# A recorder that orders a hybrid attention and DeltaNet step by a model of the engines: TensorE charged with other times

## The chip, the cores and the metric

One core of one Trainium2 chip. The metric is the device time of one execution in microseconds (us), the median of three runs. Engines: PE is TensorE, PEld its weight loads, DVE VectorE, ACT ScalarE, POOL GpSimd, SP the queue that issues DMAs.

## The reference

Two layers of a diffusion backbone over 128 context tokens and 1024 latent tokens (together 1152), D_MODEL 1024. The core of a layer:

```python
h = rms_norm(x, p['norm_g']) * (1.0 + scale) + shift
cq, ckv, kpe, gate_a, b_in, c_in, x_in, gate_b, q_in, k_in, v_in, z, a_f, a_b, b_f, b_b, merge_g = split_columns(h @ p['w_in'])
o_a = mla_attention(q_nope, q_rope, k_nope, k_rope, v) * jax.nn.silu(gate_a)
o_b = conv_branch(b_in, c_in, x_in, gate_b, p['conv_b_w'])
o_c = gdn_branch(q_in, k_in, v_in, z, a_f, a_b, b_f, b_b, h0, p)
m = s_a * (o_a @ p['w_pa']) + s_b * (o_b @ p['w_pb']) + s_c * (o_c @ p['w_pc'])
x = x + res_gate * (m @ p['w_o'])
```

`gdn_branch` is a gated delta rule in chunks of 64 tokens, eight heads, forward and backward. Its scan is a chain in which each step needs the state of the step before:

```python
def step(state, xs):
    u_i, w_i, qd_i, kd_i, at_i, gl_i = xs
    v_new = u_i - jnp.einsum('bhck,bhkv->bhcv', w_i, state)
    o_i = jnp.einsum('bhck,bhkv->bhcv', qd_i, state) + jnp.einsum('bhij,bhjv->bhiv', at_i, v_new)
    state = state * jnp.exp(gl_i)[..., None, None] + jnp.einsum('bhck,bhcv->bhkv', kd_i, v_new)
    return state, o_i
```

## The kernel before

Every value is float32; large products are split into two parts of a shorter format and made of three products (`mm3s`). A layer has three parts: the *front* (input projection, convolutions, delta rule, then the projections of the attention's queries, keys and values), the *attention* (order written out by hand, with four projection tiles as fill), and the *mix* (gates, branch projections, output projection, and the start of the next layer).

In start, front and mix the order on the engines is not written out. Each job is a stream, a generator that yields one instruction at a time (`s_ip`, `s_ga`, `s_gc`, ...). A recorder, `Flow`, holds for each engine the time at which its model thinks the engine free (`free`), and for each buffer when it was last read or written (`log`). In `run` it takes, over and over, the stream whose next instruction can start first (`max(free, ready)`, with 0.02 us per rank on top); among instructions of the same engine one of a lower rank number goes first if its wait is short. `put` then books the instruction's time and issues it. The program that comes out is fixed: each engine works through its list in order, and waits where an operand is late. The model is used while the program is built alone.

The streams that matter here:

- `ip` (rank 9, the last): the input projection, 42 tiles of 128 columns (38 in the front, the last four in attention) by three token blocks of 384, 24 whole products (128x128 by 384 columns) each. A tile is named by its place: `ip0_18_2` is layer 0, tile 18, block 2. It is what PE does when nothing else is ready. `s_w` loads and splits its weights, `s_ev` takes its results out.
- `gc` (rank 3): the chain of the scan. Jobs 0 to 3 are pairs of heads of the latent tokens with 16 steps each, job 4 the context with 2 steps. A step is four products of 64x64 by 64 columns `p1` (a state `SH` into `p1`), three DVE operations into `scr`, four `pv`, one DVE operation, four `pk`, and two DVE operations into the next `SH`. On the chip each of these products shows as two MATMUL records (x8 for four products), and the profile writes `p1` as `p`.
- `ga`, `gb`, `gz` (ranks 7, 6, 4): what a job needs ahead of its chain: decay masks (`gm`, `sg`), Gram matrices (`G`), a triangular solve of 31 steps on DVE and POOL (`tmp`, `X`), and its last part on PE (`pw`). `gd` (rank 4): the outputs (`oi`, `oa`, `ot`).
- `lb`, `ln`, `w2`: after the chains, in the tail of the front: norms (`rs_kv`, `rs_cq`) and projections `ukp`, `uvp`, `uqp`, with what is left of `ip`.

Before, PE's time of an instruction was `op.c` of `cost` alone: columns / 2400 us for a whole product of 256 columns and more, 64/1200 or 64/600 us for a 64x64 one:

```python
            if ins[0].ap[0][1] <= 64:
                t = ins[0].ap[-1][1] / (1200.0 if out.offset // out.ap[0][0] else 600.0)
            return t
```

Of the kernel before, what the change touches and what calls it, by code (L numbers as in the profile page):

```python
# [39 lines left out]


class Op:
    __slots__ = ("e", "f", "r", "w", "c", "m")


class Wait:
# [9 lines left out]
def _span(ap):  # L56
    dims = ap.ap
    if ap.space == DRAM:
        lo, p0, p1 = ap.offset, 0, 1
        rest = dims  # L60
    else:
        ps, pn = dims[0]
        p0, lo = ap.offset // ps, ap.offset % ps
        p1 = p0 + pn
        rest = dims[1:]
    hi = lo + 1
    for s, n in rest:
        if s > 0:
            hi += s * (n - 1)
        else:  # L70
            lo += s * (n - 1)
    return p0, p1, lo, hi


def _free(ap):
    n = 1
    for _, k in ap.ap[1:]:
        n *= k
    return n


class Eng:
# [7 lines left out]
    def __getattr__(self, m):  # L90
        real = getattr(self.real, m)

        def call(*a, **kw):
            if not self.k.rec:
                return real(*a, **kw)  # L95
            op = Op()
            op.e = self.e
            op.f = lambda: real(*a, **kw)  # L98
            aps = [x for x in a if hasattr(x, "tensor")]
            out = kw.get("out")  # L100
            outs = [out] if out is not None else [aps.pop(0)]
            if kw.get("accum_out") is not None:
                outs.append(kw["accum_out"])
            ins = aps + [v for n, v in kw.items() if n not in ("out", "accum_out") and hasattr(v, "tensor")]
            if m == "matmul" and not kw.get("start", True):
                ins.append(outs[0])
            op.w = [(self.k.key(x), _span(x)) for x in outs]
            op.r = [(self.k.key(x), _span(x)) for x in ins]
            op.c = self.cost(m, outs[0], ins, kw)
            op.m = ins[0].ap[-1][1] / 1200.0 if self.e == "PE" else 0.0  # L110
            return op

        return call

    def cost(self, m, out, ins, kw):
        n = max([_free(out)] + [_free(x) for x in ins if x.space != DRAM]) if self.e != "PE" else _free(out)
        if self.e == "PE":
            if m == "transpose":
                return n * 2 / 2400.0
            r = ins[1].dtype == F32R  # L120
            t = n * ((1 if n >= 256 else 4) if r else 4) / 2400.0
# [3 lines that stand above are left out]
        if self.e == "DVE":  # L125
            return (0.131 if m == "scalar_tensor_tensor" else 0.065) + n / (160.0 if m == "reciprocal" else 960.0)
        if self.e == "ACT":
            return (0.307 if ins and ins[0].space != PSUM and n > 256 else 0.13) + n / 1600.0
        if self.e == "POOL":
            if kw.get("op") == ALU.pow:  # L130
                return 0.15 + n * 0.175
            return (0.15 if m != "tensor_tensor" else 0.1) + n / (1200.0 if m != "tensor_tensor" else 475.0)
        run = 1 << 30
        for x in [out] + ins:
            c = 1
            for st, k in reversed(x.ap[0 if x.space == DRAM else 1:]):
                if st != c:
                    break
                c *= k
            run = min(run, c)  # L140
        return out.nbytes() / 360e3 * (2 if run < 128 else 1)


class Flow:
# [8 lines left out]
    def __init__(self, k):  # L153
# [3 lines left out]
        self.ev = set()  # L157
        self.pace = {}

    def ready(self, op):  # L160
        t = 0.0
        for lst, wr in ((op.r, False), (op.w, True)):
            for key, (p0, p1, lo, hi) in lst:
                ps = key[0] == "P"
                for q0, q1, l2, h2, end, eng, w in self.log.get(key, ()):
                    if eng != op.e and ps:

                        hit = (q0 // 32 < -(-p1 // 32) and p0 // 32 < -(-q1 // 32) and l2 // 512 <= (hi - 1) // 512
                               and lo // 512 <= (h2 - 1) // 512)
                    else:  # L170
                        hit = (w or wr) and q0 < p1 and p0 < q1 and l2 < hi and lo < h2
                    if hit:
                        end += self.LAG[eng, op.e]
                        if end > t:
                            t = end
        return t

    def note(self, op, end):
        for lst, w in ((op.r, False), (op.w, True)):
            for key, sp in lst:  # L180
# [5 lines left out]
                if len(recs) > 96:  # L186
                    recs.sort(key=lambda x: x[4])
                    del recs[:32]

    def put(self, op, s):  # L190
        f = self.free
        if op.e == "SP":
            f["SP"] = s + 0.06
            hw = max(s, f.get("HW", 0.0))
            f["HW"] = hw + 0.45
            d = max(hw + 1.1, f.get("DMA", 0.0))
            f["DMA"] = d + op.c
            self.note(op, d + op.c)
        else:
            if op.e == "PE":  # L200
                s = max(s, f.get("PEW", 0.0) + op.m)
                f["PEW"] = s
            f[op.e] = s + op.c
            self.note(op, s + op.c)
        op.f()

    def step(self, st):
# [22 lines left out]
    def run(self, streams, until=None, evs=()):  # L230

        for n, s in streams.items():
            if "head" not in s:
                s.update(head=None, end=False, wait=None)
        names = sorted(streams, key=lambda n: streams[n]["rank"])
        while True:
            moved = True
            while moved:
                k0 = len(self.ev)
                for n in names:  # L240
                    self.step(streams[n])
                moved = len(self.ev) != k0
            if all(streams[n]["end"] for n in (names if until is None else until)) and all(e in self.ev for e in evs):
                return
            cand = []
            for n in names:
                op = streams[n]["head"]
                if op is not None:
                    cand.append((max(self.free.get(op.e, 0.0), self.ready(op)), streams[n]["rank"], n, op))
            if not cand:  # L250
                raise RuntimeError("streams wait for each other: %s" % {n: streams[n]["wait"] for n in names})
            best = min(cand, key=lambda x: (x[0] + 0.02 * x[1], x[1]))
            for x in cand:
                if x[3].e == best[3].e and x[1] < best[1]:
                    wait = x[0] - best[0]
                    if wait <= 0 or wait < self.WIN and wait < self.PREF * (best[3].c - wait):
                        best = x
                        break
            streams[best[2]]["head"] = None
            self.put(best[3], best[0])  # L260
# [9 lines left out]
class Kern:  # L270
# [618 lines left out]
    def conv_put(self, c, put):  # L889
        RA, RB = self.cbuf["RA"], self.cbuf["RB"]  # L890
        if c == 0:
            yield put(RA[:, 1:129], 0, 128)
            yield put(RA[:, 131:387], 128, 384)
        elif c == 1:
            yield put(RA[:, 387:580], 0, 193)
            yield put(RB[:, 0:193], 191, 384)
        else:
            yield put(RB[:, 193:577], 0, 384)
# [1652 lines left out]
```

## Time and profile before

| | |
|---|---|
| median of 3 runs | 3540.32 us (3534.69 to 3552.49) |
| the profiled execution's own time | 3544.98 us |
| its span, first to last instruction | 3543.2 us |
| instructions | 65525 |
| PE busy | 3375.9 us, 95% |
| mean granted TensorE clock | 0.97 |

The span is cut by what PE does: start to 112 us, front of layer 0 to 957 us, attention and mix to 1850 us, front of layer 1 to 2692 us, then attention and mix again. The granted clock is a share of full speed, 1.0 (2.4 GHz) or 0.5 (1.2 GHz) at any time.

### The profile page before, as it was taken

The numbers are of one execution on the slowest core, as the hardware profiler recorded it, in microseconds if no ns is written. First come the engines' busy times: TensorE is split into PE (matmuls) and PEld (weight loads), VectorE is DVE, ScalarE is ACT, GpSimd is POOL, SyncE is SP. The second block draws the span as 40 slices with busy tenths as digits, with TensorE's granted clock in tenths as the row PEclk, the third lists the DMA queues.
The fourth block names the chain that finished last, engine by engine and source line by source line (L and its number), as shares of the span: only waits on it lengthen the run. The fifth ranks groups of instructions, "written<-read, shape, count | busy, mean of one in ns | idle before, by whom it ended". The sixth has DMA issues, their size and how long they took to land. (4 is left out here: it accounts for less than half of the span.)

```text
span 3543.2 us, 65525 instructions
## 1 busy us (share of the span) xinstructions
PE 3375.9 (95%) x24654; PEld 2903.7 (82%) x24654; DVE 2310.6 (65%) x5052; ACT 1187.1 (34%) x2551; POOL 1538.9 (43%) x1550
## 2 busy tenths in 40 slices
PE   7999999999899999999999999999998999999998
PEld 4988777778765699999999877777788658999998
DVE  4467776774566488856664777786455665833755
ACT  4432222223334333332444232122242443333233
POOL 3156546533157544424212645654322774444231
PEclk9999899999999999999999989999999999999999
DMA  5333213213733235466333223122256322434842
GB/s 190 98 100 77 55 54 83 59 57 122 230 83 79 51 110 162 145 203 195 123 103 107 74 75 83 47 57 73 71 187 188 73 64 70 135 100 129 256 143 87
DMA packets 381339, 389.64 MB, mean 110 GB/s; under 512 B 162016, under 2 KB 310176, under 8 KB 380640
## 3 DMA queue, kind: packets, MB, share of 16 engines
q1 hardware_dynamic: 381024, 385.46, 36.5%
q8 instruction: 195, 3.19, 0.4%
q14 instruction: 120, 0.98, 0.1%
HBM read 264.54 MB, written 120.72 MB: 109 GB/s over the span
## 5 line engine op out<-in xcount | busy, mean ns | idle before, releaser
L98 PE MATMUL ip<-h,wh_wi 128*128 128x384 f32 x5328 | 1170.5, 358 | 3.6 <-DVE gb L98 1.1
L98 PEld LDWEIGHTS ip<-h,wh_wi 128*128 128x128 f32 x5328 | 932.8, 194 | 60.1 <-issue 16.4
L95 POOL TENSOR_TENSOR acc<-acc,P 128x512 f32<-128x512 f32 x224 | 289.1, 1291 | 126.1 <-ACT P L95 110.1
L98 POOL TENSOR_TENSOR tmp<-M,X 128x2 f32<-128x2 f32 (+30 forms) x310 | 218.6, 705 | 283.4 <-DVE X L98 263.1
L95 DVE TENSOR_REDUCE mx<-s 128x1 f32<-128x384 f32 (+1 forms) x400 | 209.2, 544 | 163.9 <-PE s L95 154.5
L95 ACT ACTIVATE P<-st 128x512 f32<-128x512 f32 x292 | 173.5, 598 | 264.9 <-PE st L95 229.3
L95 PE MATMUL st<-q,K 97*128 97x512 f32 (+1 forms) x912 | 257.2, 393 | 0.0
L98 POOL TENSOR_TENSOR sl<-ss,sl 128x512 fp32r<-128x512 f32 x100 | 144.3, 1444 | 245.7 <-ACT sl L98 227.6
L98 POOL TENSOR_TENSOR wh_wi<-wri,wh_wi 128x512 fp32r<-128x512 f32 x112 | 151.9, 1366 | 155.4 <-ACT wh_wi L98 151.6
L98 PE MATMUL pp<-ob,wp 128*128 128x384 f32 x1152 | 204.1, 336 | 2.2 <-DVE ob L98 1.8
L98 DVE TENSOR_REDUCE X<-tmp 128x1 f32<-128x2 f32 (+30 forms) x620 | 184.6, 319 | 31.4 <-POOL tmp L98 23.6
L98 PEld LDWEIGHTS pp<-ob,wp 128*128 128x128 f32 x1152 | 199.1, 188 | 6.6 <-POOL ob L98 3.7
L98 PE MATMUL wop<-h,wh_wo 128*128 128x384 f32 x1152 | 202.9, 335 | 0.0
L98 PE MATMUL sg<-h,sl 128*128 128x288 f32 x1440 | 201.1, 296 | 0.1
L98 PEld LDWEIGHTS wop<-h,wh_wo 128*128 128x128 f32 x1152 | 199.7, 188 | 1.1
L98 PEld LDWEIGHTS sg<-h,sl 128*128 128x128 f32 x1440 | 194.4, 188 | 0.3 <-POOL sl L98 0.3
L98 POOL TENSOR_TENSOR mU<-mU,mt 128x384 f32<-128x384 f32 x96 | 112.6, 1173 | 182.0 <-DVE mt L98 182.0
L98 ACT ACTIVATE VT<-pv,sst 128x64 f32<-128x64 f32 x256 | 66.7, 311 | 365.4 <-DVE scr L98 349.1
L95 PEld LDWEIGHTS st<-q,K 97*128 97x128 f32 x912 | 164.0, 190 | 28.3 <-issue 11.5
L98 POOL TENSOR_TENSOR gm<-g,cst 128x256 fp32r<-128x256 f32 x144 | 107.1, 754 | 162.0 <-PE sg L98 126.3
L98 DVE TENSOR_TENSOR tmp<-M,X 128x2 f32<-128x2 f32 (+30 forms) x310 | 162.5, 524 | 18.3 <-POOL M L98 12.5
L98 DVE SCALAR_TENSOR_TENSOR ada<-wada,cs,ada 128x256 f32<-128x256 f32 x224 | 148.9, 703 | 23.2 <-DMA wada<-in_w_ada 20.7
(339 smaller groups left out, 6327.4 us busy)
## 6 DMA issues: line engine op xcount, KB each, us to landing
wri<-in_w_in SPq DMA_DIRECT2D x160, 256.0 KB, 3.4
mt<-mD SPq DMA_DIRECT2D x144, 192.0 KB, 2.9
wada<-in_w_ada SPq DMA_DIRECT2D x128, 128.0 KB, 2.3
wrp<-in_w_p SPq DMA_DIRECT2D x48, 256.0 KB, 3.6
mD<-C SPq DMA_DIRECT2D x80, 144.0 KB, 1.9
mD<-cu SPq DMA_DIRECT2D x80, 144.0 KB, 1.8
ss<-in_w_in SPq DMA_DIRECT2D x40, 256.0 KB, 4.0
ws<-in_w_in SPq DMA_DIRECT2D x40, 256.0 KB, 4.3
```

The source lines that it names most:

```text
L95: return real(*a, **kw)
L98: op.f = lambda: real(*a, **kw)
```

## The change

`Flow` no longer books `op.c` for a product, but what the new `product` says: columns / 2400 + 0.013 us from 256 columns up (at least `op.c` where that is over 0.15), 0.03, 0.08 or 0.112 us for smaller ones; 0.1 us more where a product with fewer than 128 rows or columns of weights follows one with 128, or the other way round; and twice as much where the model's interval before held less than a share `SLOW` of full work. `low`, a rule of choice, is added but is off with `LOW = 0.0`. Nothing is computed otherwise than before, and no instruction is added or removed.

```diff
@@ -40,7 +40,7 @@
 
 
 class Op:
-    __slots__ = ("e", "f", "r", "w", "c", "m")
+    __slots__ = ("e", "f", "r", "w", "c", "m", "u")
 
 
 class Wait:
@@ -108,6 +108,9 @@
             op.r = [(self.k.key(x), _span(x)) for x in ins]
             op.c = self.cost(m, outs[0], ins, kw)
             op.m = ins[0].ap[-1][1] / 1200.0 if self.e == "PE" else 0.0
+            if self.e == "PE":
+
+                op.u = (ins[0].ap[0][1], ins[0].ap[-1][1], _free(outs[0]))
             return op
 
         return call
@@ -157,6 +160,8 @@
         self.ev = set()
         self.pace = {}
 
+        self.win, self.part, self.last = {}, False, None
+
     def ready(self, op):
         t = 0.0
         for lst, wr in ((op.r, False), (op.w, True)):
@@ -186,6 +191,42 @@
                 if len(recs) > 96:
                     recs.sort(key=lambda x: x[4])
                     del recs[:32]
+
+    GRID = 3.41
+    SLOW = 0.35
+    LOW = 0.0
+    SWITCH = 0.1
+    NEAR = 0.1
+
+    @staticmethod
+    def load(op):
+
+        k, m, n = op.u
+        part = k < 128 or m < 128
+        return k * m / 16384.0 * n / 2400.0, n / 2400.0 + 0.013 if n >= 256 else 0.03 if n <= 32 else 0.08 if part else 0.112, part
+
+    def low(self, op, s):
+
+        u, t, part = self.load(op)
+        if t > 0.15 or op.w[0][0] == self.last:
+            return False
+        return u + sum(x for e, x in self.recent if e > s + t - self.GRID) < self.LOW * self.GRID
+
+    recent = ()
+
+    def product(self, op, s):
+
+        u, t, part = self.load(op)
+        t = max(t, op.c) if t > 0.15 else t
+        if part != self.part:
+            t += self.SWITCH
+        self.part, self.last = part, op.w[0][0]
+        w = int(s / self.GRID)
+        if w > 1 and self.win.get(w - 1, 0.0) < self.SLOW * self.GRID:
+            t *= 2
+        self.win[w] = self.win.get(w, 0.0) + u
+        self.recent = [x for x in self.recent if x[0] > s - self.GRID] + [(s + t, u)]
+        return s + t
 
     def put(self, op, s):
         f = self.free
@@ -200,8 +241,11 @@
             if op.e == "PE":
                 s = max(s, f.get("PEW", 0.0) + op.m)
                 f["PEW"] = s
-            f[op.e] = s + op.c
-            self.note(op, s + op.c)
+                f["PE"] = self.product(op, s)
+                self.note(op, f["PE"])
+            else:
+                f[op.e] = s + op.c
+                self.note(op, s + op.c)
         op.f()
 
     def step(self, st):
@@ -254,6 +298,12 @@
                 if x[3].e == best[3].e and x[1] < best[1]:
                     wait = x[0] - best[0]
                     if wait <= 0 or wait < self.WIN and wait < self.PREF * (best[3].c - wait):
+                        best = x
+                        break
+            if self.LOW and best[3].e == "PE" and self.low(best[3], best[0]):
+
+                for x in cand:
+                    if x[3].e == "PE" and x[0] <= best[0] + self.NEAR and self.load(x[3])[1] > 0.15:
                         best = x
                         break
             streams[best[2]]["head"] = None
```

What that does to the order is seen in three places. First PE in layer 0, job 2, the step 5 of its chain up to step 6 (`p_2_5` is `p1` of job 2, step 5; `ip_27_0` is tile 27, block 0; `sg_4_1` belongs to job 4; the numbers at the end count buffers). Before:

```order
L98 MATMUL p_2_5_6396<-SH_2_1_6076,kTb_2_5437 64x64
L98 MATMUL ip_27_0_6352<-h,wh_wi_27_6017 128x384 x7
L98 MATMUL pv_2_5_6395<-scr_2_6072,ZT_0_968 64x64
L98 MATMUL sg_4_1_6321<-gm_4_1_10_6377,mr 128x256
L98 MATMUL pv_2_5_6395<-scr_2_6072,ZT_1_969 64x64
...
L98 MATMUL ip_27_0_6352<-h,wh_wi_27_6017 128x384 x4
L98 MATMUL pk_2_5_6435<-scr_2_6072,kt_2_5442 64x64 x4
L98 MATMUL sg_4_1_6321<-gm_4_1_11_6421,mr 128x256
L98 MATMUL ip_27_0_6352<-h,wh_wi_27_6017 128x384 x2
L98 MATMUL ip_27_1_6451<-h,wh_wi_27_6017 128x384
L98 MATMUL p_2_6_6447<-SH_2_0_6075,kTb_2_5437 64x64
```

The same place now:

```order
L98 MATMUL p_2_5_5288<-SH_2_1_5112,kTb_2_4829 64x64
L98 MATMUL ip_18_2_4989<-h,wh_wi_18_3156 128x384 x2
L98 MATMUL pv_2_5_5287<-scr_2_5108,ZT_0_968 64x64
L98 MATMUL pv_2_5_5287<-scr_2_5108,ZT_1_969 64x64
...
L98 MATMUL ip_18_2_4989<-h,wh_wi_18_3156 128x384
L98 MATMUL ip_19_0_5303<-h,wh_wi_19_4403 128x384 x2
L98 MATMUL pk_2_5_5319<-scr_2_5108,kt_2_4835 64x64 x4
L98 MATMUL ip_19_0_5303<-h,wh_wi_19_4403 128x384
L98 MATMUL p_2_6_5328<-SH_2_0_5111,kTb_2_4829 64x64
```

The fourteen `ip` products and two `sg` of the step have become six `ip`, and the `ip` tile at this place is number 18 and 19 instead of 27: the chain stands earlier against the projection.

Second DVE in the same step (`scr` and `SH` are the chain's, `tmp` and `X` the triangular solve of job 3, `YA` and `YB` the convolutions). Before:

```order
L98 TENSOR_TENSOR scr_2_6072<-p_2_5_6396,sst_2_5532 128x128
L98 TENSOR_REDUCE X_3_5802<-tmp_3_5803 128x10
L98 TENSOR_TENSOR scr_2_6072<-scr_2_6072,vT_2_5438 64x128 x2
L98 TENSOR_TENSOR tmp_3_5803<-M_3_5801,X_3_5802 128x210
...
L98 TENSOR_TENSOR scr_2_6072<-pv_2_5_6395,sst_2_5532 128x128
...
L98 TENSOR_TENSOR tmp_3_5803<-M_3_5801,X_3_5802 128x242
L98 SCALAR_TENSOR_TENSOR SH_2_0_6075<-SH_2_0_6075,egl_1096,pk_2_5_6435 128x64
L98 SCALAR_TENSOR_TENSOR SH_2_1_6076<-SH_2_1_6076,egl_1096,pk_2_5_6435 128x64
```

Now:

```order
L98 TENSOR_TENSOR scr_2_5108<-p_2_5_5288,sst_2_4896 128x128
L98 TENSOR_TENSOR scr_2_5108<-scr_2_5108,vT_2_4830 64x128 x2
L98 TENSOR_TENSOR scr_2_5108<-pv_2_5_5287,sst_2_4896 128x128
L98 SCALAR_TENSOR_TENSOR SH_2_0_5111<-SH_2_0_5111,egl_1092,pk_2_5_5319 128x64
L98 SCALAR_TENSOR_TENSOR SH_2_1_5112<-SH_2_1_5112,egl_1092,pk_2_5_5319 128x64
L98 SCALAR_TENSOR_TENSOR YA_962<-RA_960,sm_122,YA_962 128x578 x2
```

Job 3's solve has left job 2's chain; in the chains of jobs 0 and 1 the next job's solve still stands.

Third PE in the tail of layer 0's front, at the first `uqp`. Before, no `ip` was left there:

```order
L98 MATMUL uqp_6_0_9730<-qn_0_8989,w_6_9611 128x384 x9
L98 MATMUL uqp_6_1_9744<-qn_1_8990,w_6_9611 128x384 x9
L98 MATMUL uqp_6_2_9762<-qn_2_8991,w_6_9611 128x384 x9
L98 MATMUL uqp_7_0_9781<-qn_0_8989,w_7_9717 128x384 x9
L98 MATMUL uqp_7_1_9795<-qn_1_8990,w_7_9717 128x384 x9
```

Now:

```order
L98 MATMUL uqp_6_0_9630<-qn_0_8658,w_6_9436 128x384 x9
L98 MATMUL ip_37_0_9615<-h,wh_wi_37_9385 128x384 x8
L98 MATMUL uqp_6_1_9662<-qn_1_8659,w_6_9436 128x384 x9
L98 MATMUL ip_37_0_9615<-h,wh_wi_37_9385 128x384 x13
L98 MATMUL ip_37_1_9688<-h,wh_wi_37_9385 128x384 x10
L98 MATMUL uqp_6_2_9706<-qn_2_8660,w_6_9436 128x384 x9
```

When the delta rule's last output stands on PE, 2305 of layer 0's 2736 `ip` products have been issued where it was 2560; in layer 1 it is 2414 where it was 2775.

## Rows read from the trace of the kernel before

**Rows 1.** The page's first part: busy us, share of the span, instructions.
```profile
PE 3375.9 (95%) x24654; PEld 2903.7 (82%) x24654; DVE 2310.6 (65%) x5052; ACT 1187.1 (34%) x2551; POOL 1538.9 (43%) x1550
```
**Rows 2.** Windows: PE, PEld, DVE, ACT, POOL busy us, clock, DMA share, GB/s.
```profile
112.00:957.00 845.00, 798.50 (x7186) 668.47 (x7185) 564.32 (x1504) 251.79 (x632) 378.14 (x455) 0.95 0.31 90
```
**Rows 3.** Windows over the eight chains, columns as above.
```profile
335.90:433.40 97.50, 93.19 (x755) 69.94 (x755) 71.53 (x169) 26.65 (x71) 50.16 (x53) 0.79 0.12 31
...
711.30:784.40 73.10, 69.24 (x695) 51.03 (x696) 53.82 (x177) 14.43 (x47) 25.56 (x34) 1.00 0.17 51
...
2318.10:2396.20 78.10, 73.56 (x746) 55.37 (x746) 68.11 (x208) 16.75 (x53) 44.45 (x57) 1.00 0.08 24
...
sum 659.70, PE 626.59 PEld 469.69 DVE 519.07 ACT 148.84 POOL 321.85; mean PE 78.32 PEld 58.71 DVE 64.88 ACT 18.60 POOL 40.23
```
**Rows 4.** The same windows, `ip` alone: PE, PEld, DVE, ACT; counts add up to 1487.
```profile
335.90:433.40 97.50, 56.75 (x187) 37.08 (x186) 0.00 (x0) 3.66 (x11) 0.79 0.12 31
465.70:542.80 77.10, 46.00 (x167) 29.10 (x166) 3.74 (x9) 1.46 (x3) 0.93 0.12 42
...
711.30:784.40 73.10, 48.76 (x192) 31.62 (x191) 3.43 (x8) 2.44 (x5) 1.00 0.17 51
...
2438.60:2515.30 76.70, 51.84 (x194) 34.77 (x193) 1.78 (x5) 2.46 (x5) 0.91 0.15 46
```
**Rows 5.** The chain that ended last, a run of whole products: start, us, what.
```profile
3423.63 36.92 PE wop L98 x213
```
**Rows 6.** Timeline of a quick step of layer 0, job 1: start, us, instruction.
```profile
473.83 0.34 PE L98 MATMUL p<-SH,kTb 64*64 64x64 f32 x8
...
475.27 0.49 PE L98 MATMUL pv<-scr,ZT 64*64 64x64 f32 x8
...
475.69 0.97 PE L98 MATMUL ip<-h,wh_wi 128*128 128x384 f32 x4
...
476.59 0.34 PE L98 MATMUL pk<-scr,kt 64*64 64x64 f32 x8
...
476.87 0.79 PE L98 MATMUL ip<-h,wh_wi 128*128 128x384 f32 x3
...
477.62 0.34 PE L98 MATMUL p<-SH,kTb 64*64 64x64 f32 x8
```
**Rows 7.** Timeline of a step of layer 0, job 0, at half clock.
```profile
387.30 0.49 PE L98 MATMUL p<-SH,kTb 64*64 64x64 f32 x8
...
390.35 0.69 PE L98 MATMUL pv<-scr,ZT 64*64 64x64 f32 x8
...
390.97 1.65 PE L98 MATMUL ip<-h,wh_wi 128*128 128x384 f32 x4
...
392.55 0.49 PE L98 MATMUL pk<-scr,kt 64*64 64x64 f32 x8
...
392.97 1.33 PE L98 MATMUL ip<-h,wh_wi 128*128 128x384 f32 x3
...
394.23 0.47 PE L98 MATMUL p<-SH,kTb 64*64 64x64 f32 x2
```
**Rows 8.** Timeline of layer 0, job 2: one set of `pv` split in two.
```profile
647.18 0.33 PE L98 MATMUL pv<-scr,ZT 64*64 64x64 f32 x2
...
647.44 0.62 PE L98 MATMUL ip<-h,wh_wi 128*128 128x384 f32 x2
...
647.99 0.44 PE L98 MATMUL pv<-scr,ZT 64*64 64x64 f32 x6
...
648.36 0.96 PE L98 MATMUL ip<-h,wh_wi 128*128 128x384 f32 x4
```
**Rows 9.** PE's waits, 842 to 957 us: us in total, times, longest.
```profile
PE rs_cq L98 <- DVE ssacq L98: 3.5, 2, 3.3
...
PE uqp L98 <- DVE hl_uq L98: 3.0, 2, 1.7
PE rs_kv L98 <- DVE rsd_kv L98: 2.4, 2, 1.5
```

## Prediction

> **What bounds the kernel now.** I read the page's first part, then the stretches of the two front stages, then each of the eight delta-rule chains in them, then single steps. The page says PE 95% busy and nothing else above 82% [rows 1]; the front of layer 0 (112 to 957 us) looks the same, 798 of 845 us [rows 2]. But this busy time counts pipelined products from issue to end, so I count products instead. An `ip` product (128x128 by 384 columns) costs 36.92/213 = 0.173 us when such products follow each other (the `wop` run has the same shape) [rows 5]. Attention keeps a fixed order, and the mix stages are such runs, so an order cannot change much there; the two fronts have gaps of another kind, and only there did many instructions move.
>
> The reader is to see this in the eight chains (layer 0 and 1, jobs 0 to 3; from the first `p` of step 0 to the first `p` of step 15, fifteen steps each). Together they last 659.7 us [rows 3] and hold 1487 `ip` products [rows 4], that is 258 us. The other 402 us, 3.35 us a step, go to the small 64x64 products, to changes between small and whole products, to waits, and to the stretches at half clock. A step cannot be short at will: it is `p`, three vector operations, `pv`, one vector operation, `pk`, two vector operations, `p` again, each behind the other. A quick one takes 477.62 - 473.83 = 3.79 us, with seven `ip` products between its `pv` and the next `p` alone [rows 6]. So the kernel's fill, about 12 `ip` a step, costs the chain little while the clock is full: whatever part of the fill is taken out of the chain must be run elsewhere at 0.173 us each, and the chain gets shorter only as far as the vector engine and this latency let it.
>
> **What the change moves.** It adds no work and removes none: 19,930 PE instructions in both programs. The recorder's model now charges 0.1 us for a change between small and whole products and doubles the PE time after an interval with little work. In that model PE is hardly free between two dependent small products, so the lowest rank, `ip`, is hardly ever chosen there. Counted in the two orders, the fifteen steps of the eight chains held 734 `ip` in layer 0 and 745 in layer 1; now they hold 47, 63, 56, 141 (307) and 44, 57, 53, 65 (219). That is 953 fewer, 953 x 0.173 = 165 us of work that runs outside the chains instead, mostly between jobs 2 and 3 and in the last part of the front.
>
> Changes between small and whole products fall from 660 to 460 in the front of layer 0 and from 658 to 452 in layer 1, so 203 round trips fewer. One round trip: eight `pv` split by two `ip` take 648.36 - 647.18 = 1.18 us [rows 8], eight unsplit ones 475.69 - 475.27 = 0.42 us [rows 6], two `ip` 0.35 us; the split cost some 0.4 us, of which part is waiting. I take 0.2 to 0.4 us, so 40 to 80 us are at stake if nothing takes the place of these changes. In a thin chain something does: PE waits for the vector engine. So I don't credit this sum; it lies inside the chain's new length.
>
> How long is a thin chain? Two limits, the later one holds. First latency. At full clock the three legs of the quick step are 1.44 + 1.32 + 1.03 us [rows 6], so 3.7 us is near the floor. At half clock `p`, `pv` and `pk` take 0.49, 0.69 and 0.49 us instead of 0.34, 0.49 and 0.34, and an `ip` adds (1.65 - 1.33) = 0.32 us [rows 7]; the leg from `pk` to `p` takes 1.68 us with three `ip`, so 1.3 with one or two (the vector operations end there then), and the leg from `pv` to `pk` 2.20 with four, so some 1.7 with two or three. With 1.6 for the leg from `p` to `pv` a thin step at half clock takes 4.6 us. Clock: the chain with 187 `ip` in 97.5 us ran at 0.79 of it, the one with 192 in 73.1 us at 1.00 [rows 3, 4]; the new ones hold 50 in some 62 us, less than any row shows, so half clock is the likelier end. I take 4.1 us, the middle between the floor and the half-clock step, because fewer products also leave less to slow down: 15 x 4.1 = 61.5 us.
>
> The Trainium skill, TensorE: Matmul & The Clock Gate, section What's actually happening, says that throttled is the default state and that activity releases it; by it every thin chain runs at half clock, and the sum below ends at its upper bound. This trace agrees that thinner chains have the lower clock, but shows none as thin.
>
> Second, the vector engine. In the new order the chains of jobs 0 and 1 still carry the next job's triangular solve (`tmp`, `X`). Adding up the vector instructions that now stand inside each chain, each with its own duration in this trace: 66, 66, 41, 54 us and 73, 58, 34, 52 us. The fullest chain before had 68.1 of 78.1 us busy, 0.87 [rows 3]. At that density: 76, 76, 47, 62 and 84, 66, 40, 60 us.
>
> So the new lengths are 76, 76, 61.5, and 66 for job 3 of layer 0 (which keeps 141 `ip`; it took 73 with 192); 84, 66, 61.5, 61.5 in layer 1: 552.5 us, 107 less than 659.7. **The sum**: -107 for the chains, +165 for the `ip` that left them. 206 small products left them too (1096 and 1094 become 992 and 992; sixteen `G` took 1.04 us where nothing held them, so 0.05 to 0.1 us each): +10. In the tail of the front, where PE waited for `rs_cq`, `rs_kv` and `uqp` [rows 9], the remaining `ip` products now stand between those; of some 22 us of listed waits in both layers (15 of them in this one) I give back 15. Handing over from one chain to the next (loads, transposes, `pw`) leaves PE idle as before, only with less fill: its latency already counted in both, 0, with 5 us to either side. Start and mix: 12 and some 180 moved PE instructions in stretches that lose little, 0. Together +53 us on the profiled execution's 3545 us: 3598 us. That execution stands 4.7 us above the median of 3540.32, so I predict 3594 us, 1.5% slower.
>
> Bounds. Lower: all steps at the 3.7 us floor and a vector engine without a gap (66, 66, 56, 60; 73, 58, 56, 56): 491 us, -169 + 165 + 10 - 22 - 5 = -21 us. Upper: 4.6 us a step and a density of 0.8: 609 us, -51 + 165 + 20 - 7 + 5 = +132 us.
>
> **Rivals.** (1) Half clock in every thin chain: the upper half of the bound, some 3650 us. For it: the clock follows the fill in all rows [rows 3, 4]; against: the vector work, not PE, sets four chains. (2) No measurable change, 3540 +- 18 us: the chains shrink by just what they lost, to some 490 to 520 us, since the steps also lose the vector work of the convolutions, which moves out with the `ip` tiles, and the saved changes pay in the mid-stretch. For it: the quick step; against: it ran at full clock. (3) Faster, some 3500 us: the place is again the chain, the mechanism the 203 round trips; at 0.2 us they give 41 us if PE never waits in their stead. It decides at a chain sum below 480 us, 4.0 us a step over all eight; but four chains hold 58 to 73 us of vector work, so it takes an almost gapless vector engine, or a tail that gives back more than the listed waits. (4) That the order changes nothing can be left out: the chains visibly differ.
>
> **How the numbers follow.** Forecast 0.45, with its own range 3560 to 3630; rival 1 0.17; rival 2 0.20; rival 3 0.18. Slower by over 0.5% (18 us, about what a measurement here can tell from no change) are the first two, 0.62; within it 0.20; faster 0.18. The range of 3512 to 3655 leaves out about half of rival 3 and part of rival 1.
>
> **What would show it.** Right: in the new profile the chains of jobs 1 and 2 last 60 to 76 us with some 60 `ip`; PE's waits for `scr` and `SH` grow from a few us a front to tens; the granted clock there falls to half; the stretch between the chains of jobs 2 and 3 is a dense run of `ip`; the tail grows. Wrong: steps of 3.7 us or less at full clock, or a front that ends at 957 us or earlier although its chains wait, which would say that changes of mode cost more than I read from the rows; or steps well over 5 us, which would say that the vector engine or the half clock costs more.

## The result, and the profile after

The changed kernel takes 3871.36 us (median, 3868.33 to 3882.09); the kernel before took 3546.40 us beside it. The ratio is 1.094, with a 95% interval of 1.0905 to 1.0972. Slower was right; 3594 us with a range to 3655 us was far too little: the loss is 325 us, not 54.

The page's first and second part, and the two fronts as windows (columns as in rows 2):

```profile
PE 3582.6 (93%) x24654; PEld 3062.9 (79%) x24654; DVE 2316.4 (60%) x5052; ACT 1191.4 (31%) x2551; POOL 1533.8 (40%) x1550
...
PEclk8997556987999999999999955599599999999999
```
```profile
112.00:1109.00 997.00, 896.70 (x7235) 750.25 (x7234) 577.96 (x1507) 255.23 (x637) 366.52 (x455) 0.80 0.27 78
1990.00:3005.00 1015.00, 929.00 (x7356) 777.82 (x7355) 574.02 (x1515) 262.97 (x649) 373.81 (x464) 0.79 0.27 79
```

DVE, ACT and POOL are busy as long as in [rows 1]; PE is "busy" 207 us longer with the same 24654 instructions. That goes with the clock: its line falls to 5 in both fronts, and their windows have 0.80 and 0.79 where the front of layer 0 had 0.95 [rows 2]. That front took 845 us and now ends 152 us later.

The chains answer to [rows 3]:

```profile
343.20:430.80 87.60, 73.61 (x620) 53.87 (x620) 59.97 (x157) 14.39 (x47) 39.83 (x49) 0.52 0.06 13
463.80:547.90 84.10, 66.73 (x527) 44.07 (x526) 63.23 (x160) 14.49 (x46) 26.27 (x27) 0.50 0.13 34
573.90:644.20 70.30, 64.06 (x528) 42.32 (x524) 34.66 (x107) 15.32 (x48) 12.75 (x11) 0.50 0.12 39
...
sum 618.70, PE 532.13 PEld 364.59 DVE 392.88 ACT 106.45 POOL 190.39; mean PE 66.52 PEld 45.57 DVE 49.11 ACT 13.31 POOL 23.80
```

and, for `ip` alone, to [rows 4]:

```profile
343.20:430.80 87.60, 22.34 (x48) 12.45 (x47) 0.55 (x1) 0.56 (x2) 0.52 0.06 13
...
828.60:900.70 72.10, 40.01 (x142) 26.20 (x141) 3.46 (x8) 1.46 (x3) 0.83 0.08 20
```

Seven of the eight chains run at 0.50 to 0.53 of the clock; only job 3 of layer 0, which kept 142 `ip`, is at 0.83. The first chain lost 139 of its 187 `ip`, 24 us of work, and became 10 us shorter. All eight together became 41 us shorter.

The hand-overs, from the last step of a chain to the next chain, were not looked at in the forecast. Here they are for layer 0 (behind jobs 0, 1, 2, 3), `ip` alone, first before, then after:

```profile
433.40:465.70 32.30, 19.95 (x75) 13.93 (x74) 0.31 (x2) 1.60 (x5) 0.89 0.46 107
542.80:594.80 52.00, 37.98 (x183) 30.99 (x183) 2.95 (x8) 1.60 (x5) 1.00 0.52 131
677.30:711.30 34.00, 23.36 (x107) 17.80 (x106) 1.80 (x5) 0.50 (x1) 1.00 0.49 120
784.40:842.20 57.80, 40.02 (x186) 31.35 (x187) 2.21 (x4) 3.88 (x8) 1.00 0.27 79
```
```profile
430.80:463.80 33.00, 6.78 (x12) 3.15 (x12) 0.00 (x0) 0.56 (x2) 0.50 0.39 76
547.90:573.90 26.00, 5.14 (x10) 2.36 (x9) 0.00 (x0) 0.56 (x2) 0.50 0.26 63
644.20:828.60 184.40, 142.91 (x701) 125.22 (x700) 10.39 (x26) 8.67 (x24) 0.93 0.25 70
900.70:957.20 56.50, 19.34 (x63) 12.33 (x64) 1.78 (x5) 0.00 (x0) 0.67 0.19 52
```

Three of the four are as empty as the chains: 444 `ip` have become 85, 62 us of work, for 26.6 us of length. The first is not shorter at all. The work piled up in the third, which grew from 34 to 184 us. PE's waits (us, times, longest) of the whole program show where PE stands in the thin stretches:

```profile
PE pv L98 <- DVE scr L98: 49.1, 65, 3.8
PE p L98 <- DVE SH L98: 31.8, 64, 2.0
PE sg L98 <- POOL gm L98: 19.7, 29, 2.8
PE adc L98 <- DVE ada L98: 18.2, 8, 7.7
```

Before they were 17.3, 9.8, 10.4 and 5.6 us. The last is no product of the front: it belongs to the mix.

**Where the 323 us between the two spans are.** Every whole product is run in either kernel, so I take from each stretch 0.173 us for each that it holds and compare what is left. The first hand-over, for instance, goes from 32.3 - 75 x 0.173 = 19.3 to 33.0 - 12 x 0.173 = 30.9 us.

| stretch | forecast, us | measured, us |
|---|---|---|
| eight chains (length, and `ip` taken out) | -107 + 165 = +58 | -41 + 165 = +124 |
| hand-overs behind jobs 0, 1, 3 | 0 | +81 |
| stretch between jobs 2 and 3 | +10 | +93 |
| ahead of the first chain | 0 | +12 |
| tails | -15 | -13 |
| start and mix | 0 | +26 |
| together | +53 | +323 (3866.5 - 3543.2) |

### The profile page after: what moved, and what is told of

It reads as the page before. It is cut to its first block, busy times and chain, and to the rows that moved or that the text cites. A ratio compares the mean times of both kernels' runs of the same rounds, so it can differ in the third digit from the quotient of the medians.

```text
span 3866.5 us, 65653 instructions
## 1 busy us (share of the span) xinstructions
PE 3582.6 (93%) x24654; PEld 3062.9 (79%) x24654; DVE 2316.4 (60%) x5052; ACT 1191.4 (31%) x2551; POOL 1533.8 (40%) x1550
## 5 line engine op out<-in xcount | busy, mean ns | idle before, releaser
L98 PE MATMUL ip<-h,wh_wi 128*128 128x384 f32 x5328 | 1216.3, 372 | 11.6 <-DVE gb L98 5.1
L98 PEld LDWEIGHTS ip<-h,wh_wi 128*128 128x128 f32 x5328 | 985.1, 204 | 76.7 <-issue 24.3
L95 PEld LDWEIGHTS st<-q,K 97*128 97x128 f32 x912 | 163.9, 190 | 28.4 <-issue 11.5
L98 PEld LDWEIGHTS pv<-scr,ZT 64*64 64x64 f32 x1152 | 96.6, 203 | 107.8 <-issue 63.1
L98 PE MATMUL pv<-scr,ZT 64*64 64x64 f32 x1152 | 126.7, 317 | 51.8 <-DVE scr L98 49.1
```

## The experiments

All but e5 and e10 change the recorder's model alone and hold the same instructions in another order. In the table, `ip` in chains counts the fifteen steps of the eight chains, `ip` in hand-overs the six behind jobs 0, 1 and 3, both in the programs' orders; the clock is that of the profiled execution.

| kernel | `ip` in chains | in hand-overs | clock | median, us | ratio to before, 95% |
|---|---|---|---|---|---|
| before | 1479 | 841 | 0.97 | 3536.0 to 3546.4 | |
| changed | 526 | 171 | 0.882 | 3871.4 | 1.0905 to 1.0972 |
| e1: no doubling | 1008 | 626 | 0.944 | 3615.2 | 1.0162 to 1.0238 |
| e2: no charge for a change | 739 | 215 | 0.891 | 3818.1 | 1.0734 to 1.0814 |
| e3: prices alone | 1329 | 760 | 0.971 | 3569.4 | 1.0035 to 1.0087 |
| e4: rule `low` on | 1445 | 785 | 0.961 | 3624.7 | 1.0182 to 1.0250 |
| e6: doubling alone | 937 | 256 | 0.909 | 3715.7 | 1.0491 to 1.0556 |
| e7: small prices alone | 1414 | 848 | 0.970 | 3525.6 | 0.9945 to 0.9986 |
| e8: `low` on old prices | 1514 | 780 | 0.967 | 3577.4 | 1.0096 to 1.0149 |
| e9: `low` for chains alone | 1538 | 523 | 0.949 | 3681.6 | 1.0370 to 1.0456 |
| e11: small prices, factor 1.2 | 1390 | 956 | 0.973 | 3528.0 | 0.9953 to 1.0004 |
| e12: small prices, charge 0.02 | 1377 | 857 | 0.972 | 3533.4 | 0.9965 to 1.0012 |

### Which of the three new charges: e1, e2, e3

```diff
-            t *= 2
+            t *= 1
```


> The changed kernel with one part undone: the recorder's model no longer doubles the PE time after a light interval; the new prices and the 0.1 us for a change of mode stay. Its order holds 1008 ip products in the eight chains (before 1479, changed 526). Theory 'fill': a chain lasts as long as its dependent steps and its vector work, whatever PE does in between, so each product taken out of it is paid again elsewhere; the changed kernel lost some 320 us for 953 products, so 471 products cost 471 x 0.34 = 160 us: 3700 us. Theory 'clock': the loss is the half clock of the thin chains; with twice as many products the clock is mostly full again and the time is within 40 us of before: 3540 to 3580 us. Theory 'other engines' (the new order of the vector and pool engines slows chains 0 and 1): the changes there remain, 3650 us or more, without relation to the count.

```diff
-    SWITCH = 0.1
+    SWITCH = 0.0
```


> The changed kernel with the charge for a change of mode at 0; the doubling and the prices stay. 739 ip products in the chains. 'Fill': 740 fewer than before, x 0.34 = 252 us: 3795 us. 'Clock': most chains stay at half clock, so about as slow as the changed kernel, 3800 to 3870 us.

The third kernel has both edits.

> The changed kernel with both undone: only the prices of the products are new. 1329 ip products in the chains. 'Fill': 150 fewer, x 0.34 = 51 us: 3595 us. 'Clock': clock as before, 3545 us. Mean clock 0.96 to 0.97 in both.

3615, 3818 and 3569 us. e1 lies outside all three of its forecasts, between clock (to 3580) and the other engines (from 3650), and far under fill (3700); e2 lies in the range of the clock theory and 23 us over the fill theory's sum; e3 lies between its two. Without the doubling 256 of the 325 us are gone, without the charge for a change of mode 53. The prices alone cost some 25 us. The slope isn't even: e1 took 686 products out of chains and hand-overs for 71 us over before, 0.10 us each (with its loss in the mix); the changed kernel took 937 more for 256 us, 0.27 us each, more than their own 0.173 us. The first products that leave are partly paid back by shorter chains; the last ones cost more than themselves.

### The rule `low`: e4

```diff
-    LOW = 0.0
+    LOW = 0.5
```


> The changed kernel with its unused rule of choice turned on (LOW = 0.5): where the model sees little work in its interval, a whole product is taken ahead of a small one. All new charges stay. 1445 ip products in the chains, 1208 changes of mode in the two fronts (before 1316, changed 910). 'Fill': 34 fewer, x 0.34 = 12 us, less 54 round trips of mode at 0.2 to 0.4 us: 3535 to 3555 us. 'Clock': clock 0.97 or more, 3520 to 3545 us. If the new charges by themselves spoil the order, it stays above 3600 us.

3625 us, neither the fill theory's sum nor the clock theory's, but the third case: the chains are filled again (1445), the clock is 0.961, and still 80 us are lost. Some 24 us of them lie in the mix, which the large prices disturb (e7); for the rest see e8 and e9.

### Half clock against lost fill: e5 and its control e10

Both put 880 products behind the chain's sets, e5 with 256 columns, e10 with 32:

```diff
+    def hot(self, n):
+        w, x = (self.h[0:128, 0, 0, 0:128], self.h[0:128, 0, 0, 0:256])
+        for _ in range(n):
+            self.core.tensor.matmul(self.pw8[0:128, 0:256], lhsT=w, rhs=x, start=True, stop=True)
...
+                self.hot(3 if not prompt else 0)
...
+                self.hot(2 if not prompt else 0)
...
+                    self.hot(2 if not prompt else 0)
```


> The order of the changed kernel, with 526 input products in the fifteen steps of the eight chains, kept as it is; added work: behind the four p, the four pv and the four pk of each step of jobs 0 to 3 stand 3, 2 and 2 products of 128x128 by 256 columns into unused PSUM columns, 880 in all, whose results nobody reads. At 256/384 of 0.173 us that is 880 x 0.115 = 101 us of pure extra work, put where PE waits for the vector engine. Theory fill (the chains are slow because their latency is idle, the half clock changes nothing): thin steps stay at 4.27 us or longer, time 3870 to 3970 us. Theory clock (half the loss is that PE runs at half clock in the thin stretches): the granted clock of the chains goes from half to full, thin steps go from 4.27 to 3.7 to 3.9 us, the eight chains from 619 to 540 to 580 us, and the time FALLS by 40 to 80 us, to 3790 to 3830, although work is added. If the granted clock stays at half in the chains, the run tells neither.

> The run with 880 extra whole products once more, but each of 32 columns in place of 256: the same count at the same places of the program, little work in each; results unused again. If it was the clock that shortened the thin steps there from 4.27 to 3.57 us: the granted clock of the chains of jobs 1 and 2 is half as in the changed kernel and the thin steps stay at 4.27 us or a little more; time 3870 to 3900 us. If it was something else about extra products (a changed mode of the array ahead of the small ones, other weights): thin steps of 3.6 to 3.9 us at half clock.

3893.8 us for e5 (ratio 1.0974 to 1.1074, clock 0.913) and 3988.8 us for e10 (1.1244 to 1.1353, clock 0.871). As a total e5 fell inside the fill theory's 3870 to 3970 us and missed the clock theory's 3790 to 3830. But the clock came back in part of the chains only. e10 is far above the 3870 to 3900 us that I had expected. Windows of e5 over job 0 and job 2 of layer 0 and job 2 of layer 1:

```profile
345.60:448.60 103.00, 100.09 (x721) 77.34 (x720) 56.18 (x151) 13.94 (x44) 37.85 (x46) 0.52 0.05 11
592.60:658.60 66.00, 59.87 (x636) 43.69 (x631) 34.20 (x107) 15.14 (x48) 12.75 (x11) 0.90 0.13 42
2470.70:2529.60 58.90, 56.31 (x628) 41.02 (x625) 29.06 (x101) 11.40 (x43) 9.37 (x9) 0.99 0.09 29
```

Where the clock stayed at 0.52 the added work made the chain 15 us longer (87.6 to 103.0). Where it rose, the chain became shorter although it holds 105 products more: 70.3 to 66.0 and 66.6 to 58.9 us. A plain step of layer 1, job 2: step 6 of the chain in the changed kernel and in e5, step 5 in e10, whose step 6 takes 5.45 us too (start, us, instruction; line 414 is the added one, in unused columns of `pw`):

```profile
2453.90 0.49 PE L98 MATMUL p<-SH,kTb 64*64 64x64 f32 x8
2454.32 1.01 PE L98 MATMUL ip<-h,wh_wi 128*128 128x384 f32 x2
2455.26 0.86 PE L98 MATMUL pv<-scr,ZT 64*64 64x64 f32 x8
...
2456.99 0.49 PE L98 MATMUL pk<-scr,kt 64*64 64x64 f32 x8
2457.41 0.69 PE L98 MATMUL ip<-h,wh_wi 128*128 128x384 f32 x1
2458.16 0.49 PE L98 MATMUL p<-SH,kTb 64*64 64x64 f32 x8
```
```profile
2494.06 0.34 PE L98 MATMUL p<-SH,kTb 64*64 64x64 f32 x8
2494.34 0.62 PE L414 MATMUL pw<-h 128*128 128x256 f32 x3
2494.79 0.52 PE L98 MATMUL ip<-h,wh_wi 128*128 128x384 f32 x2
2495.24 0.65 PE L98 MATMUL pv<-scr,ZT 64*64 64x64 f32 x8
...
2496.61 0.34 PE L98 MATMUL pk<-scr,kt 64*64 64x64 f32 x8
...
2497.64 0.34 PE L98 MATMUL p<-SH,kTb 64*64 64x64 f32 x8
```
```profile
2538.60 0.49 PE L98 MATMUL p<-SH,kTb 64*64 64x64 f32 x8
2539.02 0.82 PE L414 MATMUL pw<-h 128*128 128x32 f32 x3
2539.68 0.99 PE L98 MATMUL ip<-h,wh_wi 128*128 128x384 f32 x2
...
2544.05 0.49 PE L98 MATMUL p<-SH,kTb 64*64 64x64 f32 x8
```

The step lasts 4.26 us at half clock, 3.58 us at full clock with seven products more, and 5.45 us with seven small ones at half clock. The control shows that added products by themselves lengthen the step, so 4.26 - 3.58 = 0.68 us is the least that half clock costs it. Over the whole chain: before it took 78.1 us with 195 `ip` at full clock [rows 3]; with 142 fewer, 24.6 us of work, it takes 66.6 us at half clock, 11.5 less, and 58.9 us in e5, 19.2 less, although the added products stand in it. And the eight chains of e5 last 641.6 us, those of e10 731.4 us, with as many products at the same places, and e5's are the larger ones. Both theories hold a part. If all 120 steps paid 0.68 us, that would be 82 us; and by the table above 199 of the 323 us lie outside the chains, so half clock in the chains is not the whole loss. The Trainium skill, TensorE: Matmul & The Clock Gate, section What's actually happening, says that activity releases the throttle; e5 agrees, since work that nobody needs took the clock from 0.50 to 0.99 in one chain, and e10, with as many instructions and little work, didn't.

### The doubling by itself: e6, and a small factor: e11

```diff
-    SWITCH = 0.1
+    SWITCH = 0.0
...
-        t = max(t, op.c) if t > 0.15 else t
+        t = op.c
```


> Before's prices, no charge for a change of mode, only the doubling of the time after a thin interval of the model: 937 input products stay in the fifteen steps of the eight chains (1479 before, 526 in the changed kernel), 64 to 71 of them in each of the chains of jobs 1 and 2. Theory fill (each product taken out costs its 0.173 us): 3545 + 542 x 0.173 = 3639 us. Theory clock (a chain with 60 to 70 products falls to half clock, and its hand-over with it): four of the eight chains thin, so about half of the changed kernel's 325 us, plus the hand-overs: 3700 to 3800 us, mean clock 0.90 to 0.94. Rival that the doubling needs the switch charge to do harm: under 3600.

3715.7 us, as the clock theory said: the doubling by itself costs 5% (1.0491 to 1.0556), some 180 us; on top of the other new charges it was 256. Here four chains are thin (jobs 1 and 2) and four are not, in one kernel. Chains of jobs 1, 2 and 3 of layer 0:

```profile
463.50:552.00 88.50, 81.95 (x617) 58.61 (x614) 67.86 (x217) 15.73 (x50) 50.55 (x66) 0.52 0.18 46
579.80:665.50 85.70, 79.17 (x611) 55.49 (x611) 62.51 (x212) 15.06 (x48) 49.20 (x69) 0.50 0.15 37
710.80:781.20 70.40, 66.73 (x667) 49.49 (x668) 53.25 (x159) 15.66 (x50) 24.68 (x29) 1.00 0.14 40
```

The two thin ones hold 70 and 64 `ip` where before they held 166 and 191, run at half clock, and are longer than before: 88.5 and 85.7 for 77.1 and 82.5 us. The full one is no longer than before. So these chains gave away 17 and 22 us of work and got longer.

e11 has the prices of e7 (below), no charge for a change of mode, and a factor of 1.2:

```diff
-    SWITCH = 0.1
+    SWITCH = 0.0
...
-        t = max(t, op.c) if t > 0.15 else t
+        t = op.c if op.u[2] >= 256 else t
...
-            t *= 2
+            t *= 1.2
```


> New prices for small products, old ones for large products, no charge for a change of mode, and a factor of 1.2 in place of 2 behind a thin interval: 1390 input products in the chains, 956 in the three hand-overs (1414 and 848 with factor 1, which took 3525.6 us), 1134 in the tails (1020). Theory fill: the moves cancel, 3525 +- 10. If hand-overs are worth more to fill than chains: 3505 to 3520. If the factor harms at any size: over 3540.

3528.0 us: a factor of 1.2 costs nothing that can be told from e7's factor 1 (3525.6 us), and every chain keeps 159 to 196 `ip`. I read this as follows from the code, without a run of its own: in the model a doubled chain leaves PE no time before the next chain product, `ip` with the last rank isn't taken, the interval stays thin, and the doubling confirms itself; 1.2 isn't enough for that.

### The prices of small and of large products: e7, and a small charge: e12

e7 is e11's edit with `t *= 1`.

> Only the prices of the small products are the new ones; products of 256 columns and more keep their old price, no charge for a change of mode, no doubling: 1414 input products in the chains. If the 25 us that all new prices together cost (3569) come from the 0.013 us on each large product, which moves the adaLN products in the mix: 3535 to 3550 us, and the sg stages return to 261 and 245 us. If they come from the small prices: 3565 to 3575. Better prices as a gain: under 3527.

3525.6 us, ratio 0.9945 to 0.9986: the lower bound of the gain is 0.14%, the upper 0.55%, so a little faster than before. From e3 it differs in the price of the large products alone, and the ratios are 0.95% apart, 34 us. They lie in the mix. Its `sg` stage of layer 0 in the changed kernel, as a window and PE's waits there:

```profile
1440.20:1716.20 276.00, 256.76 (x1850) 252.09 (x1849) 196.99 (x365) 98.78 (x208) 108.33 (x76) 0.98 0.44 138
```
```profile
PE adc L98 <- DVE ada L98: 9.7, 6, 5.7
PE sg L98 <- POOL sl L98: 7.4, 9, 2.0
```

The same in e7:

```profile
1285.20:1537.60 252.40, 246.82 (x1850) 245.90 (x1849) 199.62 (x362) 95.29 (x206) 106.64 (x74) 1.00 0.48 150
```
```profile
PE sg L98 <- POOL sl L98: 4.1, 2, 2.2
PE adc L98 <- DVE ada L98: 1.4, 1, 1.4
```

With 0.013 us more on each large product the order puts the `adc` products in places where their operand `ada` isn't there yet. These waits account for about half of the difference (17.1 against 5.5 us); PE is also busy 10 us longer with the same 1850 products, which I didn't take apart. The stage takes 276.0 us (280.2 in e3); with the old price 252.4, before 261.4.

e7 also gives the price of an emptied hand-over. Behind job 1 of layer 0 it has 61 `ip` at full clock:

```profile
547.60:576.50 28.90, 27.30 (x475) 21.50 (x474) 12.32 (x46) 10.55 (x32) 19.64 (x21) 1.00 0.40 92
```

In the changed kernel the same hand-over has 10 `ip` and takes 26.0 us at 0.50: 51 products fewer, 8.8 us of work, for 2.9 us of length. In e1 it holds 45 `ip`, also at 1.00, and takes 25.5 us (530.2 to 555.7 us): no longer than with 10.

e12 is e7 with a small charge (the line is shown against the changed kernel):

```diff
-    SWITCH = 0.1
+    SWITCH = 0.02
```


> New prices for small products, old ones for large products, no doubling, and a charge of 0.02 us for a change of mode in place of 0.1: 1377 input products in the chains, 857 in the three hand-overs, 1120 changes between small and whole products in the fronts (1130 with no charge at 3525.6 us, 1316 in before). Theory fill: 37 products fewer in the chains, +6: 3525 to 3535 us. If changes of mode are worth saving: below 3520.

3533.4 us, not told apart from before. Changes of mode are 1120 instead of 1316, as in e7 (1130).

### Filling by force: e8 and e9

e8 is the kernel before with the rule on: it has the old prices and no charge by the edit of e6, no doubling (`t *= 1`), and this line:

```diff
-    LOW = 0.0
+    LOW = 0.35
```


> Before's prices, no charge, no doubling; only the rule low is on, with LOW = 0.35: a whole product is taken ahead of a small one when the model's last interval held under 35% of full work. 1514 input products in the chains (1479 before). Theory clock: some of the 213 us at half clock of before go, mean clock over 0.98, 3500 to 3535 us. Theory fill alone: 35 x 0.173 = 6 us less, 3540. If the products put ahead delay the chain: 3560 or more.

e9 is e4 with the rule for the chain's stream alone:

```diff
-            if self.LOW and best[3].e == "PE" and self.low(best[3], best[0]):
+            if self.LOW and best[3].e == "PE" and best[2] == "gc" and self.low(best[3], best[0]):
```


> The changed kernel with the rule low turned on (LOW = 0.5), but for the chain's own stream gc alone: 1538 input products in the fifteen steps of the eight chains (526 in the changed kernel, 1479 in before), but the hand-overs behind the chains of jobs 0, 1 and 3 keep only 523 (171 in the changed kernel, 841 in before, 785 with the rule on for all streams, which took 3624.7 us) and the tails of the two fronts 1703 (before 1059). Theory that a hand-over's idle time is the same with or without fill and costs nothing more (the forecast's zero): 3600 to 3625 us. Theory that each product missing from a hand-over costs its 0.173 us as in a chain: 3625 + 262 x 0.173 - 93 x 0.173 = 3640 to 3660 us.

3577.4 and 3681.6 us. In e8 the chains hold 35 `ip` more than before and by the account above cost 15 us less; so they aren't delayed, which is what I had expected behind a time over 3560 us. But the tail of layer 0 runs dry: 355 whole products where there were 494. First before, then e8:

```profile
842.20:957.30 115.10, 100.34 (x544) 92.38 (x544) 65.72 (x134) 50.69 (x110) 20.89 (x18) 0.97 0.61 202
```
```profile
862.60:977.50 114.90, 90.67 (x405) 78.33 (x404) 59.71 (x128) 45.58 (x100) 14.75 (x14) 0.81 0.55 183
```

As long with 139 products fewer, 24 us (12 more in layer 1): the tail waits for its norms, and now less covers that. e9 ends 20 us above the dearer of my two sums. Its hand-overs hold 318 `ip` fewer than before and cost some 39 us by the account above, in sign what the fill theory says, and most of its size (318 x 0.173 = 55); but its chains, fuller than before, cost 45 us more, which neither theory had. Its job 1 of layer 0:

```profile
472.10:575.10 103.00, 89.83 (x822) 69.12 (x822) 71.88 (x197) 20.14 (x58) 50.54 (x71) 0.83 0.18 49
```

103.0 us with 202 `ip`, for 77.1 with 167 [rows 4]. What the rule does there I can't say for certain: it puts whole products ahead of chain products that were ready, and the chain holds more of the next job's small products.

## Why the prediction was wrong

**Right:** the direction, and what it rests on: 953 `ip` leave the chains for 165 us, and the chains don't get shorter by as much. Also the signs to look for: PE's waits for `scr` and `SH` in the tens, half clock in the thin chains, a dense run between jobs 2 and 3, longer tails. The tails gave back 13 us for a forecast of 15. What a round trip is worth stays unknown: e12 has 98 fewer than before and can't be told from it, but it also has 102 `ip` fewer in its chains, up to 18 us of work, so the two may cancel.

**The step that failed first: "Handing over from one chain to the next ... 0, with 5 us to either side".** It was argued that the idle time was counted in both kernels. But 670 `ip` left the hand-overs, and the sum counted only the 953 of the chains: 116 us of work for 35 us of length, +81 us. The orders showed it; I had counted the chains alone. In its place: a stretch that is filled counts like a chain, whatever runs in it.

**The dense run between jobs 2 and 3** was taken as a place where `ip` costs its 0.173 us and nothing else. It cost 93 us beyond that, 83 more than forecast. The preparation of jobs 3 and 4 now runs there with no chain beside it. In layer 0 the loss is 47.7 us. PE is idle for 184.4 - 168.9 = 15.5 us of the stretch, against 1.0 before; the clock of 0.93 adds some 13; and 168 small products of the preparation (`G`, `sg`, `kq`), none of which stood there before, are busy some 20 us (6.5, 7.8 and 6.2). Their records overlap those of others, so this is an estimate, but it about fills the loss. The +10 us that the forecast gave to all 206 small products was too little: these alone take 0.12 us each.

**The lengths of the chains** came out 66 us above the forecast 552.5. The plain thin step was off by little: 4.1 us forecast, 4.26 measured, half clock throughout where I took the middle; and half clock itself was read too dear (4.6; the leg from `p` to `pv` took 1.36 us for 1.6). That the clock followed the fill "in all rows" was not quite so: 194 `ip` in 76.7 us had 0.91 where 167 in 77.1 had 0.93 [rows 4]. Half of the 66 us lies in jobs 2 and 3, 67 to 75 us for a forecast of 61.5 and 66, where not every step is plain: steps with other small products beside the chain's took 5 to 7 us. The other half lies in jobs 0 and 1, 79 to 88 us for a forecast of 66 to 84. They were sized as vector-bound at a density of 0.87, but the vector engine is busy only 0.68 and 0.75 of the first two (59.97 of 87.60 us, 63.23 of 84.10), so by its busy time it isn't the limit; its work, forecast as 66 us in both, was itself counted high. Half clock has a part in it: job 1 of layer 0 takes 84.9 us in e5, at 0.75 of the clock, and 95.1 us in e10, at 0.50. That PE at half clock and DVE take turns there is argued from the small products of the next job that both carry, not shown.

**Start and mix** were set to 0 because the moved instructions lie "in stretches that lose little". The `sg` stages lost 28 us (261.4 to 276.0 and 245.2 to 258.9), and e7, with the old price of the large products alone, has them back (252.4 us in layer 0): that price is the cause.

The rivals: half clock in every thin chain was the right mechanism for seven of the eight, but with 3650 us it had the same omissions. No change and faster fell. What stays open is how the hand-overs' 81 us divide between lost fill and half clock. Two runs speak for lost fill: e1's hand-over above, as long with 45 `ip` at full clock as with 10 at half; and e5, where the six have the same `ip` and in five of them the clock is 0.06 to 0.16 higher (0.60 to 0.73), yet together they take 237.8 us for 235.8, with some 3.5 us of added products in them. No run has an empty one at full clock. Open is also why the rule `low` harms filled chains.

## What to carry to other kernels

Before pricing a reordering, count the fill in every stretch between two long dependences, not only in the one that the change aims at, and charge what leaves at its full time unless that stretch visibly gets shorter. A model that makes an engine slower when it is idle can keep it idle: such a charge needs a choice that can answer it (e4 got back 247 of 325 us), or a small factor (e11). A price nearer to the measured one isn't a better order: 0.013 us on a large product cost the mix some 34 us between e7 and e3, in part by where a late operand was met.

## What was not expected of the hardware

Work that nobody needs shortened a chain: 105 added products of 256 columns, 58.9 us for 66.6, with the clock at 0.99 for 0.50. And at half clock a whole product of 32 columns isn't cheap: three take 2539.68 - 2539.02 = 0.66 us, 0.22 us each. The weight load beside each is itself longer than that (least, median and longest ns of one, with the product below it, e10):

```profile
L414 PEld LDWEIGHTS pw<-h x75: 286/333/333, 2512.1 to 2569.5; 128*128 128x128 f32 x75
L414 PE MATMUL pw<-h x75: 374/374/393, 2512.1 to 2569.6; 128*128 128x32 f32 x75
```

At full clock in e5 the same load takes 188 ns (median).
